# Rotary embedding on one core: TensorE tiles in three groups, a third buffer for the sin product, tables on the queue of x

## The chip, the cores and the metric

The kernel runs on one core of a Trainium2 chip. The core has a matrix engine (TensorE, PE in the profile), a vector engine (VectorE, DVE), a scalar engine (ScalarE, ACT), a general engine (GpSimd, POOL) and SyncE (SP), which here only starts transfers. They share two on-chip memories, SBUF and PSUM; data come from the chip's large memory (HBM) through 16 DMA engines. GpSimd does not touch PSUM in this kernel; TensorE writes only to it. The metric is the device time of one execution in microseconds (us), the median over runs.

## The reference

```python
x: (8, 2048, 8, 64) f32      # batch, position, head, feature
cos, sin: (2048, 32) f32     # one row for each position
x1 = x[..., :32];  x2 = x[..., 32:]
out1 = x1 * cos - x2 * sin   # cos, sin repeated over batch and heads
out2 = x1 * sin + x2 * cos
return concatenate([out1, out2], axis=-1)
```

Each half of a head's 64 features is multiplied by cos, the other half by sin (with a minus sign for the first), and the two products are added. x and the result are 33.55 MB each, the tables 0.26 MB each.

## The kernel before, in words

The 2048 positions are spread over the 128 partitions, 16 to a partition. A *pair* is eight positions of one batch for all partitions (128 x 4096 floats, 2 MB); there are 16 pairs, and each is loaded by one transfer and stored by one. Only the first load and the last store are cut in two. A pair consists of two *tiles* of 128 x 2048 floats, so there are 32 tiles, numbered 0 to 31; pair p holds tiles 2p and 2p + 1. All loads of x are issued by SyncE in the order of the pairs, into a ring of ten pair buffers (xpool). The result is written over x in the same buffer and the store is issued by ScalarE's queue (L155; L151 and L153 for the last two halves), so a buffer comes free for a later load when its store has landed.

The tables are loaded by ScalarE's queue (L56, L57). VectorE makes ssin from sin, once with and once without the minus sign (L80, L81), and copies cos to PSUM (L82); ScalarE copies sin to PSUM (L83). GpSimd makes an identity matrix (eye), ScalarE a negative one (neye).

A tile is done in one of three ways, which the table `kinds` gives by its number:

- **A** (all others): GpSimd makes the sin product t2 in two halves (L118), VectorE the cos product t1 in PSUM (L123), VectorE adds them (L129).
- **B** (6, 9, 14, 16, 21, 27): GpSimd makes t2 as in A, VectorE makes t1 in SBUF (L123); TensorE adds them by multiplying each with the identity into one PSUM buffer (L134, L135), in four chunks of 512; ScalarE copies each chunk to the tile's place (L136).
- **C** (3, 11, 18, 24): VectorE makes both products (L111 for sin, L123 for cos); TensorE adds them with eye or neye and with the halves exchanged (L143, L144); ScalarE copies (L147). GpSimd has no part in it.

The rings: t2 has two SBUF buffers for all kinds; t1 of A has one PSUM buffer; t1 of B and C (tag t1s) has two SBUF buffers; the PSUM chunks o of TensorE have two. A buffer comes free when its last reader is done: the add for A, the last matmuls for B and C.

Order: each engine runs its own queue in order and waits by semaphores. A planner sets the order of every queue when the program is built: it goes by the loop's order, but moves an instruction ahead of one that it expects to wait, and it fixes which buffer each tile gets. So the order in the trace isn't exactly that of the loop, and a wait for a buffer is a wait for one given earlier reader.

Of the kernel before, what the change touches and what calls it, by code (L numbers as in the profile page):

```python
# [2 lines left out]

# [4 lines left out]


@with_exitstack  # L10
def kernel(
    ctx: ExitStack,
    tc: tile.TileContext,
    x: bass.AP,
    cos: bass.AP,
    sin: bass.AP,
    out: bass.AP,
):
    nc = tc.nc
    f32 = mybir.dt.float32  # L20
    PSUM = bass.MemoryType.PSUM

    B, S, H, D = x.shape
    Dh = D // 2
    P = 128
    HD = H * D
    R = S // P

    SL = 4
    FREE = SL * HD  # L30
    PAIR = 2 * FREE
    n_pair = R // (2 * SL)
    C = 512

    xv = x.rearrange("b (q r) h d -> b q (r h d)", q=P)
    ov = out.rearrange("b (q r) h d -> b q (r h d)", q=P)
    cos_src = cos.rearrange("(q r) d -> q r d", q=P)
    sin_src = sin.rearrange("(q r) d -> q r d", q=P)

    const_pool = ctx.enter_context(tc.tile_pool(name="const", bufs=1))  # L40
    tab_pool = ctx.enter_context(tc.tile_pool(name="tab", bufs=1, space=PSUM))
    t1_pool = ctx.enter_context(tc.tile_pool(name="t1p", bufs=1, space=PSUM))
    o_pool = ctx.enter_context(tc.tile_pool(name="op", bufs=2, space=PSUM))
    xpool = ctx.enter_context(tc.tile_pool(name="xpool", bufs=10))
    t1s_pool = ctx.enter_context(tc.tile_pool(name="t1s", bufs=2))
    t2_pool = ctx.enter_context(tc.tile_pool(name="t2p", bufs=2))

    cos_sb = const_pool.tile([P, R, Dh], f32, tag="cb")
    sin_sb = const_pool.tile([P, R, Dh], f32, tag="sb")
    ssin = const_pool.tile([P, R, 2, Dh], f32, tag="ss")  # L50
    eye = const_pool.tile([P, P], f32, tag="eye")
    neye = const_pool.tile([P, P], f32, tag="neye")
    cos_ps = tab_pool.tile([P, R, Dh], f32, tag="cp")
    sin_ps = tab_pool.tile([P, R, Dh], f32, tag="sp")

    nc.scalar.dma_start(out=sin_sb, in_=sin_src)  # L56
    nc.scalar.dma_start(out=cos_sb, in_=cos_src)  # L57

    pairs = [(b, l) for l in range(n_pair) for b in range(B)]
    xts = []  # L60
    for i, (b, l) in enumerate(pairs):
        xt = xpool.tile([P, PAIR], f32, tag="xt", name=f"xt{i}")
        for lo, n in [(0, FREE), (FREE, FREE)] if i == 0 else [(0, PAIR)]:
            nc.sync.dma_start(
                out=xt[:, lo : lo + n],
                in_=xv[b, :, l * PAIR + lo : l * PAIR + lo + n],
            )
        xts.append(xt)

    nc.gpsimd.memset(eye, 0.0)  # L70
    nc.gpsimd.affine_select(
        out=eye,
        in_=eye,
        compare_op=mybir.AluOpType.not_equal,
        fill=1.0,
        base=0,
        pattern=[[-1, P]],
        channel_multiplier=1,
    )
    nc.vector.tensor_scalar_mul(ssin[:, :, 0, :], sin_sb, -1.0)  # L80
    nc.vector.tensor_copy(ssin[:, :, 1, :], sin_sb)  # L81
    nc.vector.tensor_copy(cos_ps, cos_sb)  # L82
    nc.scalar.copy(sin_ps, sin_sb)  # L83
    nc.scalar.mul(neye, eye, -1.0)

    def rep(a, n):
        return dataclasses.replace(a, ap=[a.ap[0][:], a.ap[1][:], [0, n], a.ap[-1][:]])

    kinds = {3: "C", 11: "C", 18: "C", 24: "C", 6: "B", 9: "B", 14: "B", 16: "B", 21: "B", 27: "B"}
    n_tiles = 2 * len(pairs)  # L90

    for i in range(n_tiles):
        b, l = pairs[i // 2]
        pt = xts[i // 2]
        half = i % 2
        xt = pt[:, half * FREE : (half + 1) * FREE]
        r0 = (2 * l + half) * SL
        kind = kinds.get(i, "A")
        xk = xt.rearrange("p (r k d) -> p r k d", r=SL, d=Dh)
        xu = xt.rearrange("p (g u d) -> p g u d", u=2, d=Dh)  # L100

        t2 = t2_pool.tile([P, FREE], f32, tag="t2")
        t2u = t2.rearrange("p (g u d) -> p g u d", u=2, d=Dh)
        if kind == "A":
            t1 = t1_pool.tile([P, FREE], f32, tag="t1")
        else:
            t1 = t1s_pool.tile([P, FREE], f32, tag="t1s")
        t1u = t1.rearrange("p (g u d) -> p g u d", u=2, d=Dh)

        if kind == "C":  # L110
            nc.vector.tensor_mul(  # L111
                out=t2.rearrange("p (r k d) -> p r k d", r=SL, d=Dh),
                in0=xk,
                in1=rep(sin_ps[:, r0 : r0 + SL, :], 2 * H),
            )
        else:
            for u in range(2):
                nc.gpsimd.tensor_mul(  # L118
                    out=t2u[:, :, u, :].rearrange("p (r h) d -> p r h d", h=H),
                    in0=xu[:, :, 1 - u, :].rearrange("p (r h) d -> p r h d", h=H),  # L120
                    in1=rep(ssin[:, r0 : r0 + SL, u, :], H),
                )
        nc.vector.tensor_mul(  # L123
            out=t1.rearrange("p (r k d) -> p r k d", r=SL, d=Dh),
            in0=xk,
            in1=rep(cos_ps[:, r0 : r0 + SL, :], 2 * H),
        )
        if kind == "A":
            nc.vector.tensor_add(out=xt, in0=t1, in1=t2)  # L129
        elif kind == "B":  # L130
            for j in range(FREE // C):
                o = o_pool.tile([P, C], f32, tag="o")
                cs = slice(j * C, (j + 1) * C)
                nc.tensor.matmul(o, eye, t1[:, cs], start=True, stop=False)  # L134
                nc.tensor.matmul(o, eye, t2[:, cs], start=False, stop=True)  # L135
                nc.scalar.copy(xt[:, cs], o)  # L136
        else:
            G = C // Dh
            for u in range(2):
                for j in range(FREE // 2 // C):  # L140
                    o = o_pool.tile([P, C], f32, tag="o")
                    gs = slice(j * G, (j + 1) * G)
                    nc.tensor.matmul(o, eye, t1u[:, gs, u, :], start=True, stop=False)  # L143
                    nc.tensor.matmul(  # L144
                        o, eye if u else neye, t2u[:, gs, 1 - u, :], start=False, stop=True
                    )
                    nc.scalar.copy(xu[:, gs, u, :], o.rearrange("p (g d) -> p g d", d=Dh))  # L147

        base = l * PAIR
        if i == n_tiles - 2:  # L150
            nc.scalar.dma_start(out=ov[b, :, base : base + FREE], in_=xt)  # L151
        elif i == n_tiles - 1:
            nc.scalar.dma_start(out=ov[b, :, base + FREE : base + PAIR], in_=xt)  # L153
        elif half:
            nc.scalar.dma_start(out=ov[b, :, base : base + PAIR], in_=pt)  # L155


# [1 line left out]
_INS = ['x', 'cos', 'sin']  # L159
_OUTS = [((8, 2048, 8, 64), 'float32')]  # L160


# [23 lines left out]
```

## Time and profile before

| | before |
|---|---|
| median of 3 runs | 194.11 us (193.7 to 194.29) |
| the profiled execution | 196.04 us |
| its span, first to last instruction | 194.3 us |
| VectorE busy | 132.9 us (68%) |
| GpSimd busy | 129.7 us (67%) |
| TensorE busy, mean granted clock | 91.8 us (47%), 0.789 |
| ScalarE busy | 25.2 us (13%) |
| bytes moved | 67.68 MB, mean 348 GB/s over the span |

The profile is of one execution. Its page gives busy time by engine; the span in 40 equal slices of 4.86 us with the DMA rate of each; the chain of work that ended last; groups of instructions by source line (busy time, mean, idle time before them and what ended it); and the DMA issues. A line is named L118 for line 118 of the kernel as printed above. In a group's row, `t<-xt,ssin` is what is written and what is read, with buffer numbers left out, so t1 and t2 both appear as t. Busy times that lie beside each other on different engines do not add up; idle time of an engine matters only where the chain passes through it.

### The profile page before, as it was taken

To read this page: it belongs to the slowest core of one execution; us is meant where nothing else is said; L and a number is where in the kernel's file an instruction comes from. 1 tells how busy PE (TensorE), PEld (TensorE's weight loads), DVE (VectorE), ACT (ScalarE), POOL (GpSimd) and SP (SyncE) were. 2 spreads that over 40 slices of the span, in tenths; PEclk is the share of its full clock that TensorE was granted. 3 is DMA by queue.
4 is the path that set the end of the run, shared out by engine and by line. 5 is a ranking of instruction groups with operands and counts; after the bars stand their busy time and mean duration, and the time that the engine had idled before them with its cause. 6 is when DMAs were issued, how large, how long until landed. Compare 5 with 4: busy or idle time off the path is not lost. (4 is left out here: it accounts for less than half of the span.)

```text
span 194.3 us, 670 instructions
## 1 busy us (share of the span) xinstructions
PE 91.8 (47%) x160; PEld 36.2 (19%) x160; DVE 132.9 (68%) x61; ACT 25.2 (13%) x43; POOL 129.7 (67%) x62
## 2 busy tenths in 40 slices
PE   0000009949342999026969991159149508900000
PEld 0000004414011343012424340024024103300000
DVE  0199999981996394994581979906999960955940
ACT  2100001302200222020222231011023101102000
POOL 1599345998659636859598459595972689559900
PEclk9999999996955599855796999658859965885555
DMA  6999999999999999999999999990069950008596
GB/s 208 439 432 428 378 432 432 432 432 432 432 432 432 432 432 432 432 432 432 432 428 428 432 427 428 430 398 7 2 253 418 405 219 0 0 0 378 216 432 270
DMA packets 5189, 67.68 MB, mean 348 GB/s; under 512 B 577, under 2 KB 577, under 8 KB 833
## 3 DMA queue, kind: packets, MB, share of 16 engines
q10 hardware_dynamic: 2736, 34.08, 41.3%
q1 hardware_dynamic: 2448, 33.56, 41.0%
q8 instruction: 1, 0.02, 0.0%
q14 instruction: 4, 0.02, 0.0%
HBM read 34.08 MB, written 33.55 MB: 348 GB/s over the span
## 5 line engine op out<-in xcount | busy, mean ns | idle before, releaser
L118 POOL TENSOR_TENSOR t<-xt,ssin 128x1024 f32<-128x1024 f32 x56 | 129.0, 2332 | 53.8 <-DVE xt L129 39.4
L129 DVE TENSOR_TENSOR xt<-t,t 128x2048 f32<-128x2048 f32 x22 | 50.4, 2292 | 43.8 <-POOL t L118 43.4
L123 DVE TENSOR_TENSOR t<-xt,cos_ps 128x2048 f32<-128x2048 f32 x32 | 72.4, 2290 | 0.6
L135 PE MATMUL o<-t,eye 128*128 128x512 f32 x48 | 33.7, 797 | 23.5 <-POOL t L118 23.5
L134 PE MATMUL o<-t,eye 128*128 128x512 f32 x48 | 32.4, 767 | 18.9 <-DVE t L123 10.6
L143 PE MATMUL o<-t,eye 128*128 128x512 f32 x32 | 19.0, 679 | 35.5 <-DVE t L123 29.0
L136 ACT COPY xt<-o 128x512 f32<-128x512 f32 x24 | 13.8, 586 | 92.1 <-PE o L135 75.2
L135 PEld LDWEIGHTS o<-t,eye 128*128 128x128 f32 x48 | 11.2, 246 | 42.2 <-POOL t L118 29.9
L134 PEld LDWEIGHTS o<-t,eye 128*128 128x128 f32 x48 | 11.5, 251 | 37.1 <-issue 27.0
L147 ACT COPY xt<-o 128x512 f32<-128x512 f32 x16 | 9.3, 586 | 53.7 <-PE o L144 43.2
L143 PEld LDWEIGHTS o<-t,eye 128*128 128x128 f32 x32 | 6.8, 219 | 43.8 <-issue 36.5
L144 PE MATMUL o<-t,neye 128*128 128x512 f32 x16 | 9.7, 696 | 0.5 <-DVE t L111 0.5
L111 DVE TENSOR_TENSOR t<-xt,sin_ps 128x2048 f32<-128x2048 f32 x4 | 9.1, 2287 | 0.3
L144 PE MATMUL o<-t,eye 128*128 128x512 f32 x16 | 8.2, 593 | 0.0
L80 DVE TENSOR_SCALAR ssin<-sin_sb 128x512 f32<-128x512 f32 x1 | 0.4, 427 | 6.6 <-DMA sin_sb<-in_sin_dram 6.6
L144 PEld LDWEIGHTS o<-t,neye 128*128 128x128 f32 x16 | 3.6, 232 | 6.1 <-issue 3.7
L144 PEld LDWEIGHTS o<-t,eye 128*128 128x128 f32 x16 | 3.0, 190 | 3.8 <-issue 3.8
L82 DVE COPY cos_ps<-cos_sb 128x512 f32<-128x512 f32 x1 | 0.7, 695 | 2.4 <-DMA cos_sb<-in_cos_dram 2.4
L83 ACT ACT_TABLE_LOAD x1 | 1.3, 1283 | 1.7 <-PEq L170 1.7
L83 ACT COPY sin_ps<-sin_sb 128x512 f32<-128x512 f32 x1 | 0.6, 590 | 3.7 <-DMA sin_sb<-in_sin_dram 3.7
L81 DVE COPY ssin<-sin_sb 128x512 f32<-128x512 f32 x1 | 0.4, 421 | 0.0
L70 POOL MEMSET eye<- 128x128 f32 x1 | 0.2, 204 | 0.3 <-POOLq L170 0.3
(6 smaller groups left out, 1.0 us busy)
## 6 DMA issues: line engine op xcount, KB each, us to landing
xt<-in_x_dram SPq DMA_DIRECT2D x15, 2048.0 KB, 32.4
out_dram<-xt ACTq DMA_DIRECT2D x15, 2048.0 KB, 14.3
xt<-in_x_dram SPq DMA_DIRECT2D x2, 1024.0 KB, 7.0
out_dram<-xt ACTq DMA_DIRECT2D x2, 1024.0 KB, 5.2
sin_sb<-in_sin_dram ACTq DMA_DIRECT2D x1, 256.0 KB, 5.8
cos_sb<-in_cos_dram ACTq DMA_DIRECT2D x1, 256.0 KB, 8.6
```

Source lines behind the costliest of these rows:

```text
L82: nc.vector.tensor_copy(cos_ps, cos_sb)
L83: nc.scalar.copy(sin_ps, sin_sb)
L111: nc.vector.tensor_mul(out=t2.rearrange("p (r k d) -> p r k d", r=SL, d=Dh), in0=xk, in1=rep(sin_ps[:, r0 : r0 + SL, :], 2 * H),)
L118: nc.gpsimd.tensor_mul(out=t2u[:, :, u, :].rearrange("p (r h) d -> p r h d", h=H), in0=xu[:, :, 1 - u, :].rearrange("p (r h) d -> p r h d" ...
L123: nc.vector.tensor_mul(out=t1.rearrange("p (r k d) -> p r k d", r=SL, d=Dh), in0=xk, in1=rep(cos_ps[:, r0 : r0 + SL, :], 2 * H),)
L129: nc.vector.tensor_add(out=xt, in0=t1, in1=t2)
L134: nc.tensor.matmul(o, eye, t1[:, cs], start=True, stop=False)
L135: nc.tensor.matmul(o, eye, t2[:, cs], start=False, stop=True)
L136: nc.scalar.copy(xt[:, cs], o)
L143: nc.tensor.matmul(o, eye, t1u[:, gs, u, :], start=True, stop=False)
L144: nc.tensor.matmul(o, eye if u else neye, t2u[:, gs, 1 - u, :], start=False, stop=True)
L147: nc.scalar.copy(xu[:, gs, u, :], o.rearrange("p (g d) -> p g d", d=Dh))
```

## The change

The ten TensorE tiles become nine, in three groups of consecutive tiles: a C tile (5, 13, 21) with two B tiles behind it (6, 7; 14, 15; 22, 23). t2 gets a third buffer, and so does the ring t1s; a C tile's sin product takes its buffer from t1s and no longer from t2. The ring of x goes from ten pair buffers to nine. The two table loads are issued by SyncE, ahead of the loads of x, and no longer by ScalarE's queue.

```diff
-    xpool = ctx.enter_context(tc.tile_pool(name="xpool", bufs=10))
-    t1s_pool = ctx.enter_context(tc.tile_pool(name="t1s", bufs=2))
-    t2_pool = ctx.enter_context(tc.tile_pool(name="t2p", bufs=2))
+    xpool = ctx.enter_context(tc.tile_pool(name="xpool", bufs=9))
+    t1s_pool = ctx.enter_context(tc.tile_pool(name="t1s", bufs=3))
+    t2_pool = ctx.enter_context(tc.tile_pool(name="t2p", bufs=3))
...
-    nc.scalar.dma_start(out=sin_sb, in_=sin_src)
-    nc.scalar.dma_start(out=cos_sb, in_=cos_src)
+    nc.sync.dma_start(out=sin_sb, in_=sin_src)
+    nc.sync.dma_start(out=cos_sb, in_=cos_src)
...
-    kinds = {3: "C", 11: "C", 18: "C", 24: "C", 6: "B", 9: "B", 14: "B", 16: "B", 21: "B", 27: "B"}
+    kinds = {}
+    for g in (5, 13, 21):
+        kinds |= {g: "C", g + 1: "B", g + 2: "B"}
...
-        t2 = t2_pool.tile([P, FREE], f32, tag="t2")
+        if kind == "C":
+            t2 = t1s_pool.tile([P, FREE], f32, tag="t1s", name="t2c")
+        else:
+            t2 = t2_pool.tile([P, FREE], f32, tag="t2")
```

## The prediction

> **What bounds the kernel now.** I read the page's head and slices first, then the engines' waits, the timelines of GpSimd, VectorE and TensorE, and last a table of DMA by stretches.
>
> ```profile
> span 194.3 us, 670 instructions
> PE 91.8 (47%) x160; PEld 36.2 (19%) x160; DVE 132.9 (68%) x61; ACT 25.2 (13%) x43; POOL 129.7 (67%) x62
> GB/s 208 439 432 428 378 432 432 432 432 432 432 432 432 432 432 432 432 432 432 432 428 428 432 427 428 430 398 7 2 253 418 405 219 0 0 0 378 216 432 270
> DMA packets 5189, 67.68 MB, mean 348 GB/s; under 512 B 577, under 2 KB 577, under 8 KB 833
> POOL 23%; issue 10%; DVE 9%; POOLq 1%; DVEq 0%
> ```
>
> No engine is busy over 68% of the span. The DMA row is flat near 432 until about 126 us (26 slices of 4.86) and then has holes: in the first part transfers fill the time, in the last third they wait for results. The chain that ended last is GpSimd and VectorE in turn, with 10% "issue" between. Who waits for whom (engine and line, waited for: total us, times, longest):
>
> ```profile
> DVE xt L129 <- POOL t L118: 43.4, 17, 7.0
> POOL t L118 <- DVE xt L129: 39.4, 14, 5.8
> ```
>
> The add (L129) waits for the sin product of its tile (L118), and the next sin product waits for an add. The second wait is a buffer's: t2 has two, and a tile for TensorE holds one for long, so GpSimd and VectorE share the other in turns. In time:
>
> ```profile
> 7.11 13.84 POOL L118 TENSOR_TENSOR t<-xt,ssin 128x1024 f32<-128x1024 f32 x6 [5.81 <-DVE ssin L80]
> 116.69 4.62 POOL L118 TENSOR_TENSOR t<-xt,ssin 128x1024 f32<-128x1024 f32 x2 [2.40 <-DVE xt L129]
> 123.71 9.18 POOL L118 TENSOR_TENSOR t<-xt,ssin 128x1024 f32<-128x1024 f32 x4 [2.40 <-DVE xt L129]
> 15.23 2.29 DVE L123 TENSOR_TENSOR t<-xt,cos_ps 128x2048 f32<-128x2048 f32 x1
> 19.95 2.29 DVE L123 TENSOR_TENSOR t<-xt,cos_ps 128x2048 f32<-128x2048 f32 x1
> 22.16 2.28 DVE L111 TENSOR_TENSOR t<-xt,sin_ps 128x2048 f32<-128x2048 f32 x1
> 24.36 2.28 DVE L129 TENSOR_TENSOR xt<-t,t 128x2048 f32<-128x2048 f32 x1
> 116.65 4.49 DVE L123 TENSOR_TENSOR t<-xt,cos_ps 128x2048 f32<-128x2048 f32 x2
> 121.34 2.29 DVE L129 TENSOR_TENSOR xt<-t,t 128x2048 f32<-128x2048 f32 x1 [0.21 <-POOL t L118]
> ```
>
> Columns: start, length, engine, line, operation, count, idle time before it with its releaser. A tile costs GpSimd 4.62 (two halves). Started alone it goes 116.69 to 123.71, 7.02 a tile: 4.62, then 2.40 for the add. Two facts for later: an ordinary tile costs VectorE 19.95 - 15.23 = 4.72 when multiply and add alternate, two multiplies in a row 4.49; and the instruction order isn't that of the loop: one multiply of a coming TensorE tile (L111 at 22.16, the second L123 at 116.65) stands ahead of an add.
>
> **The change part by part.** *Floor of the transfers.* Bytes stay the same.
>
> ```profile
> 0.00:2.50 2.50, 0.00 (x0) 0.00 (x0) 0.00 (x0) 0.85 (x1) 0.70 (x6) 1.00 0.33 52
> 2.50:122.00 119.50, 64.18 (x114) 25.34 (x114) 87.98 (x42) 17.56 (x31) 83.07 (x36) 0.86 1.01 428
> 192.50:194.30 1.80, 0.00 (x0) 0.00 (x0) 0.00 (x0) 0.00 (x0) 0.00 (x0) 0.50 0.02 5
> ```
>
> The last columns are the granted clock, DMA share and GB/s. From 2.5 us on 428 GB/s, and some 1.7 us after the last bytes. 67.68 MB less 0.13 at 428 is 157.8; with 2.5 and 1.7 the span cannot be below about 162.0. At the flat 432 it is 160.6. The Trainium skill ("DMA: Bandwidth & Descriptors", section Bandwidth) says that between HBM and on-chip memory the HBM side binds, near 358 GB/s; by it 67.68 MB take 189 us and the change could win almost nothing. The trace disagrees: 428 over 119.5 us.
>
> *Groups.* Tiles 3, 11, 18, 24 (C: both products on VectorE) and 6, 9, 14, 16, 21, 27 (B: sin product on GpSimd) become 5, 13, 21 (C) and the two behind each (B): nine instead of ten. GpSimd's products go from 56 to 58, +4.6 us. VectorE keeps 58 large operations (23 x 2 + 3 x 2 + 6, before 22 x 2 + 4 x 2 + 6). TensorE loses 16 matmuls and ScalarE 4 copies: nothing by themselves, with 47% and 13% busy.
>
> *Buffers.* The third t2, and C's sin product moved to the t1s ring (three), so that only B tiles hold t2. Without any waits GpSimd would need 7.1 + 29 x 4.62 = 141.1, the last add 2.3 more: 143.4. VectorE: first add at 7.1 + 4.62 = 11.7, so a start of 9.3; 23 x 4.72 + 6 x 2.25 (C) + 6 x 2.25 (B) = 135.6; end 144.9. VectorE is later, by little.
>
> ```profile
> 184.30 2.29 DVE L129 TENSOR_TENSOR xt<-t,t 128x2048 f32<-128x2048 f32 x1
> 186.63 0.34 ACTq L153 DMA_DIRECT2D out_dram<-xt  x1
> ```
>
> From the last add's end (186.59) to the end of the span it is 7.7 now; so 144.9 + 7.7 = 152.6 plus stalls S. The floor of 162.0 hides the first 9.4 us of S.
>
> *Stalls of a group.* TensorE's time for a tile:
>
> ```profile
> 28.98 2.05 PE L143 MATMUL o<-t,eye 128*128 128x512 f32 x2 [28.98 <-DVE t L123]
> 38.32 1.96 PE L134 MATMUL o<-t,eye 128*128 128x512 f32 x4
> 70.86 1.02 PE L143 MATMUL o<-t,eye 128*128 128x512 f32 x2
> 76.86 1.02 PE L144 MATMUL o<-t,eye 128*128 128x512 f32 x2
> ```
>
> 9.3 after a rest (rows start as 2.05), 7.0 right behind another tile. Take group 5, 6, 7, with time 0 where the add of tile 4 ends, and sin5 ahead of that add, as at 22.16 above. cos5 0 to 2.3; TensorE has tile 5 until 11.6. GpSimd: tile 6 from -2.3 to 2.3, tile 7 to 6.9, tile 8 (third buffer) to 11.5. cos6 to 4.5, cos8 to 6.8; cos7 has no t1s buffer, since tile 5 has two of three until 11.6. Then either add8 first (11.5 to 13.8), or cos7 first (11.6 to 13.9) and add8 to 16.2. Tile 9 wants to start at 11.5, but tiles 6 and 7 hold their t2 (6 leaves TensorE at 18.6, 7 at 25.6), so it starts at add8's end: 13.8 or 16.2. Tile 10 gets tile 6's buffer at 18.6 against 18.4, or has no wait. Loss 2.5 or 4.7 a group, 7.5 or 14.1 for three. If cos5 too is issued behind other work (TensorE until 13.9), the same steps give 4.6 with add8 first, 7.0 with cos7 first, and in the loop's strict order (cos7, cos8, add8) 9.2: 13.8, 21 and 27.6 for three. With both multiplies of C early by one more operation the loss is at most 2.3, 7 for three. Which order is issued no row of before shows. I take 14: one multiply ahead is what the trace has nearly everywhere, and cos7 becomes ready within 0.1 us of add8. Ends: 7 and 28.
>
> Sum: 152.6 + 14 = 166.6, with the floor at 162.0 beneath it.
>
> *Tables ahead of x on SP.*
>
> ```profile
> xt<-in_x_dram SPq DMA_DIRECT2D x15, 2048.0 KB, 32.4
> xt<-in_x_dram SPq DMA_DIRECT2D x2, 1024.0 KB, 7.0
> sin_sb<-in_sin_dram ACTq DMA_DIRECT2D x1, 256.0 KB, 5.8
> cos_sb<-in_cos_dram ACTq DMA_DIRECT2D x1, 256.0 KB, 8.6
> 0.73 0.40 ACTq L56 DMA_DIRECT2D sin_sb<-in_sin_dram  x1
> 19.95 0.35 ACTq L155 DMA_DIRECT2D out_dram<-xt  x1
> 9.78 0.69 DVE L82 COPY cos_ps<-cos_sb 128x512 f32<-128x512 f32 x1 [2.41 <-DMA cos_sb<-in_cos_dram]
> ```
>
> Now the tables share the engines with x and cos lands last, so VectorE's first multiply is at 10.5. Two issues (some 0.4 us each) and 0.52 MB (1.2 us at 428) go ahead of x's first half: it lands up to 2.0 later than now, or no later, since those bytes also competed with it before. GpSimd's start: 7.1, bounds 6 to 9. VectorE starts 2 to 3 us sooner, but its first add waits for GpSimd at 11.7 (now 12.9). I take 0 beyond the 11.7 that is in the sum. ScalarE's queue loses two issues that nothing waited behind.
>
> *Ring of x from 10 to 9.* Pair 9's load now waits for pair 0's store (now issued at 19.95); GpSimd reaches pair 9 near 7.1 + 16 x 4.62 = 81, some 60 us later: I take nothing, unless loads come late at the end. With both queues sharing 432, a pair takes 9.7 us; from some 20 us (four pairs in) twelve more end near 136. Pair 15 then needs 2 x 4.62 + 2.3 and the tail of 7.7: 155, under the floor. If that cover goes, each us late counts fully beyond 162.
>
> **The rivals.**
>
> ```profile
> L118 POOL TENSOR_TENSOR t<-xt,ssin 128x1024 f32<-128x1024 f32 x56 | 129.0, 2332 | 53.8 <-DVE xt L129 39.4 <-issue 8.4 <-DVE ssin L80 5.8
> ACT xt L147 <- DVE xt L129: 10.5, 1, 10.5
> ACT xt L136 <- DVE xt L129: 16.9, 2, 8.7
> ```
>
> (1) Transfers bind alone: S stays under 9.4, and the span is 162. For it: 26 flat slices, two waits of 40 us attacked. Against: S must be 3 a group or less. (2) cos7 stands ahead of add8 while TensorE is still on tile 5: S 21 to 28, span 173 to 180. For it: tile 5 takes two of three t1s buffers, and a resting TensorE needs 9.3. Against: multiplies are seen moved forward, around waits. (3) Slower: B tiles hold the added buffer as well. TensorE gets three tiles in a row, 9.3 + 7.0 + 7.0, so two of three t2 are held much of the time, and every other tile goes at 7.02. If GpSimd's idle time behind the start stays as it is (53.8 less 5.8), the 4.6 of the added tile come on top: 194.3 + 4.6 = 199. It decides from 42 us of idle on. Against: by the steps above both are held only from 2.3 to 18.6 in a group of 37 us, two tiles' worth. (4) The two other rows: three times ScalarE's copies stood 8 to 10.5 behind a store that waited for an add, and TensorE with them. Once in each group on the way to tile 6's release, up to 10.5 more a group: 166.6 + 31 = 198, no gain. Against it: the store behind a group (tiles 8 and 9) comes after that group's copies in the loop. (5) The rate falls to the span's mean of 348 with loads and stores mixed throughout: 67.68/0.348 + 4.2 = 199. Against it: the kernel mixes them from 20 us on without a fall. The 358 of the Trainium skill's DMA page would give 193 in the same way.
>
> **How the numbers follow.** The forecast, S between 9.4 and 18, is 0.42 and spans 162 to 171. Rival 1 is 0.24, rival 2 is 0.23, rivals 3 and 4 are 0.04 each, rival 5 is 0.03. Predicted: 166.6 on the span. The profiled execution took 196.04 with a span of 194.3; the median of the runs, 194.11, is 0.2 under the span, so 166.4. The range goes from 160.5 (flat 432) to 179 (rival 2) and leaves out rivals 3 to 5 (0.11) and the worst of rival 2, some 0.15 together. About 0.3% is what a measurement here can tell from no change. Faster: forecast, rivals 1 and 2, a part of 4: 0.91. Same 0.02, slower 0.07.
>
> **What would show it.** GpSimd's waits for L129 fall from 39.4 to under 15, and what is left stands behind tiles 8, 16 and 24. DMA stays near 430 until past 150 us. VectorE has no wait for L118 over 3 us outside the groups. L118 shows x58 with the same 2.33 us. cos_ps is copied before 7 us. The prediction is wrong if 7.02 remains the pace of ordinary tiles, if L123 shows idle time for TensorE over 5 us a group, or if DMA has holes with x still to be loaded.

## The result and the profile after

The changed kernel takes 176.36 us (median of 4 runs, 175.32 to 177.09) against 194.2 us for the kernel before in the same series: a ratio of 0.9065, 95% interval 0.8993 to 0.9136. It is 17.8 us faster, and 10.0 us slower than the 166.4 that was forecast, inside the range of 160.5 to 179. Medians are over all runs of a version and ratios over its fast runs; of the four runs of each version that has all stores on SyncE (below) one was slow, which raises its median by 0.4 to 0.6 us.

In the changed kernel the lines have other numbers: L123 is GpSimd's sin product, L128 VectorE's cos product, L134 the add, L139, L140 and L141 the two matmuls and the copy of a B tile, L148, L149 and L152 those of a C tile, L160 a store. In the changed kernel with the old tile numbers they are two lower (L121 for the sin product, L132 for the add). From the page of the changed kernel: the head, busy time by engine, the DMA rate in 40 slices of 4.38 us, the chain.

```profile
span 175.3 us, 632 instructions
PE 79.5 (45%) x144; PEld 32.4 (18%) x144; DVE 132.7 (76%) x61; ACT 22.5 (13%) x39; POOL 134.0 (76%) x64
GB/s 176 331 443 426 426 378 445 419 430 430 441 434 422 426 434 445 426 430 422 437 441 419 434 421 437 441 419 428 430 432 437 366 202 0 419 60 359 419 419 239
POOL 58%; issue 18%; DVE 14%; DMA 4%; SPq 0%; DVEq 0%; POOLq 0%
```

Busy time is what it was: VectorE 132.7 (132.9 before), GpSimd 134.0 (129.7, one more tile). The rate is flat until 136 us (31 slices) and holes come only then. So the gain is idle time between GpSimd and VectorE. The longest waits of the changed kernel (who, for what: us in total, times, longest):

```profile
ACT xt L141 <- DVE xt L134: 68.0, 7, 10.7
PE o L139 <- ACT xt L141: 37.7, 6, 7.8
POOL t L123 <- DVE xt L134: 21.2, 6, 7.5
DVE xt L134 <- POOL t L123: 15.4, 8, 2.4
DVE t L128 <- PE o L148: 9.5, 3, 5.1
```

GpSimd's waits for an add fell from 39.4 to 21.2, VectorE's for a sin product from 43.4 to 15.4. New are VectorE's wait for TensorE (a buffer of t1s) and, at the head of the list, ScalarE's copies behind something that waits for an add: 68.0 in seven waits, three waits with 27.4 before. The timeline of GpSimd, whole from the first product on:

```profile
9.58 36.59 POOL L123 TENSOR_TENSOR t<-xt,ssin 128x1024 f32<-128x1024 f32 x16 [8.27 <-DMA xt<-in_x_dram]
53.66 4.63 POOL L123 TENSOR_TENSOR t<-xt,ssin 128x1024 f32<-128x1024 f32 x2 [7.50 <-DVE xt L134]
60.69 27.77 POOL L123 TENSOR_TENSOR t<-xt,ssin 128x1024 f32<-128x1024 f32 x12 [2.40 <-DVE xt L134]
92.59 4.60 POOL L123 TENSOR_TENSOR t<-xt,ssin 128x1024 f32<-128x1024 f32 x2 [4.13 <-DVE xt L134]
99.60 27.77 POOL L123 TENSOR_TENSOR t<-xt,ssin 128x1024 f32<-128x1024 f32 x12 [2.40 <-DVE xt L134]
129.77 4.59 POOL L123 TENSOR_TENSOR t<-xt,ssin 128x1024 f32<-128x1024 f32 x2 [2.40 <-DVE xt L134]
136.77 27.51 POOL L123 TENSOR_TENSOR t<-xt,ssin 128x1024 f32<-128x1024 f32 x12 [2.40 <-DVE xt L134]
```

In four of the seven stretches it now makes six or eight tiles without a stop, where 7.02 a tile was the pace before. Two waits are left behind each group: 7.50 and 2.40, 4.13 and 2.40, 2.40 and 2.40. The first group on VectorE, TensorE and ScalarE:

```profile
37.11 2.28 DVE L134 TENSOR_TENSOR xt<-t,t 128x2048 f32<-128x2048 f32 x1
39.31 2.28 DVE L128 TENSOR_TENSOR t<-xt,cos_ps 128x2048 f32<-128x2048 f32 x1
46.70 4.49 DVE L128 TENSOR_TENSOR t<-xt,cos_ps 128x2048 f32<-128x2048 f32 x2 [5.10 <-PE o L148]
51.29 2.29 DVE L134 TENSOR_TENSOR xt<-t,t 128x2048 f32<-128x2048 f32 x1
...
37.34 2.05 PE L148 MATMUL o<-t,eye 128*128 128x512 f32 x2 [37.34 <-DVE t L128]
45.64 1.02 PE L148 MATMUL o<-t,eye 128*128 128x512 f32 x2
53.36 1.02 PE L140 MATMUL o<-t,eye 128*128 128x512 f32 x2
61.66 2.08 PE L139 MATMUL o<-t,eye 128*128 128x512 f32 x2 [5.56 <-ACT xt L141]
75.29 1.92 PE L140 MATMUL o<-t,eye 128*128 128x512 f32 x2
...
60.65 0.34 ACTq L160 DMA_DIRECT2D out_dram<-xt  x1
61.03 1.07 ACT L141 COPY xt<-o 128x512 f32<-128x512 f32 x2 [7.74 <-DVE xt L134]
72.40 0.34 ACTq L160 DMA_DIRECT2D out_dram<-xt  x1
72.78 1.07 ACT L141 COPY xt<-o 128x512 f32<-128x512 f32 x2 [10.69 <-DVE xt L134]
```

TensorE starts on tile 5 at 37.34, before add4 is over (39.39). After cos6 (39.31) VectorE stands until TensorE has read cos5 for the last time (45.64 and 1.02 more); then come cos7 and cos8 (46.70, two multiplies), then add8 (51.29), which releases the buffer for tile 9 at 53.66. GpSimd had been done with tile 8 at 46.17. TensorE is done with tile 6 at 54.4, but tile 10 starts at 60.69, when add9 is over: the planner had given it tile 9's buffer, not tile 6's, which had been free for 4 us when GpSimd was done with tile 9 at 58.29. The semaphores in the trace bear this out: tile 10's product waits for VectorE's, tile 11's for TensorE's. And tile 7, begun at 54.2, stays on TensorE until 77, because its chunks' copies stand on ScalarE's queue behind two stores (60.65, 72.40) that wait for the adds of tiles 9 and 11.

### The profile page after: what moved, and what is told of

It reads as the page before. It is cut to its first block, busy times and chain, and to the rows that moved or that the text cites. A ratio compares the mean times of both kernels' runs of the same rounds, so it can differ in the third digit from the quotient of the medians.

```text
span 175.3 us, 632 instructions
## 1 busy us (share of the span) xinstructions
PE 79.5 (45%) x144; PEld 32.4 (18%) x144; DVE 132.7 (76%) x61; ACT 22.5 (13%) x39; POOL 134.0 (76%) x64
## 4 chain that ended last, share of the span: by engine, by line
POOL 58%; issue 18%; DVE 14%; DMA 4%; SPq 0%; DVEq 0%; POOLq 0%
POOL t L123 58%; DVE xt L134 8%; DVE t L128 7%; DMA xt<-in_x_dram 4%; SPq L57 0%; SPq L56 0%; DVEq L134 0%; POOLq L123 0%
## 5 line engine op out<-in xcount | busy, mean ns | idle before, releaser
L123 POOL TENSOR_TENSOR t<-xt,ssin 128x1024 f32<-128x1024 f32 x58 | 133.3, 2342 | 29.7 <-DVE xt L134 21.2
L128 DVE TENSOR_TENSOR t<-xt,cos_ps 128x2048 f32<-128x2048 f32 x32 | 72.8, 2291 | 14.8 <-PE o L148 9.5
L134 DVE TENSOR_TENSOR xt<-t,t 128x2048 f32<-128x2048 f32 x23 | 52.7, 2290 | 16.6 <-POOL t L123 15.4
L139 PE MATMUL o<-t,eye 128*128 128x512 f32 x48 | 32.7, 771 | 37.7 <-ACT xt L141 37.7
L148 PE MATMUL o<-t,eye 128*128 128x512 f32 x24 | 14.6, 695 | 37.6 <-DVE t L128 37.6
L140 PE MATMUL o<-t,eye 128*128 128x512 f32 x48 | 29.5, 702 | 0.0
L141 ACT COPY xt<-o 128x512 f32<-128x512 f32 x24 | 13.4, 588 | 83.4 <-DVE xt L134 68.0
L139 PEld LDWEIGHTS o<-t,eye 128*128 128x128 f32 x48 | 10.9, 242 | 53.5 <-ACT xt L141 42.8
L140 PEld LDWEIGHTS o<-t,eye 128*128 128x128 f32 x48 | 11.3, 236 | 15.9 <-issue 15.9
L152 ACT COPY xt<-o 128x512 f32<-128x512 f32 x12 | 7.0, 586 | 51.3 <-PE o L149 51.3
L148 PEld LDWEIGHTS o<-t,eye 128*128 128x128 f32 x24 | 5.1, 224 | 45.2 <-POOL t L123 37.3
L149 PE MATMUL o<-t2c,neye 128*128 128x512 f32 x12 | 7.5, 713 | 0.0
L116 DVE TENSOR_TENSOR t2c<-xt,sin_ps 128x2048 f32<-128x2048 f32 x3 | 6.8, 2280 | 0.0
L149 PE MATMUL o<-t2c,eye 128*128 128x512 f32 x12 | 6.1, 592 | 0.0
L149 PEld LDWEIGHTS o<-t2c,neye 128*128 128x128 f32 x12 | 2.9, 239 | 4.1 <-issue 4.1
L149 PEld LDWEIGHTS o<-t2c,eye 128*128 128x128 f32 x12 | 2.3, 190 | 2.9 <-issue 2.9
```

Source lines behind the costliest of these rows:

```text
L116: nc.vector.tensor_mul(out=t2.rearrange("p (r k d) -> p r k d", r=SL, d=Dh), in0=xk, in1=rep(sin_ps[:, r0 : r0 + SL, :], 2 * H),)
L123: nc.gpsimd.tensor_mul(out=t2u[:, :, u, :].rearrange("p (r h) d -> p r h d", h=H), in0=xu[:, :, 1 - u, :].rearrange("p (r h) d -> p r h d" ...
L128: nc.vector.tensor_mul(out=t1.rearrange("p (r k d) -> p r k d", r=SL, d=Dh), in0=xk, in1=rep(cos_ps[:, r0 : r0 + SL, :], 2 * H),)
L149: nc.tensor.matmul(o, eye if u else neye, t2u[:, gs, 1 - u, :], start=False, stop=True)
```

## The experiments

The theory after the result: the third t2 buffer brings the gain, and the forecast's gap is the wait for a t1s buffer inside a group (VectorE's 9.5 and what follows). Its rivals: the grouping brings the gain; the gap is due to buffers fixed to the wrong reader, to the stores on ScalarE's queue, or to the start.

**Two t2 buffers again.**

```diff
-    t2_pool = ctx.enter_context(tc.tile_pool(name="t2p", bufs=3))
+    t2_pool = ctx.enter_context(tc.tile_pool(name="t2p", bufs=2))
```

> The changed kernel with two t2 buffers again; C's sin product stays in the t1s ring. Theory (the third t2 buffer carries the gain): the two B tiles of a group hold both buffers, so the tile behind them waits until TensorE leaves the first B tile, some 12 to 14 us later, and the next tile 2.4 more: about 15 us a group in place of the 4.8 to 9.9 seen, so 194 to 200 us, and GpSimd's waits for buffers 42 to 50 us in place of 21. Rival (grouping and the separate place of C's product carry it): 176 to 180.

192.51 us, ratio to before 0.9881 (0.9807 to 0.9956). The gain is nearly all gone, and the rival is wrong; the time is 1.5 us below the theory's range. GpSimd's stop in the first group, TensorE's last row of tile 6, and all three stops together:

```profile
54.00 4.66 POOL L123 TENSOR_TENSOR t<-xt,ssin 128x1024 f32<-128x1024 f32 x2 [10.03 <-issue]
52.84 1.02 PE L140 MATMUL o<-t,eye 128*128 128x512 f32 x2
POOL t L123 <- issue: 29.8, 3, 10.0
```

One stop of some 10 us a group, and 2.4 more behind it: 12.4 in place of the 15 expected. The profile names no releaser, but the first stop ends at 54.00, just after TensorE's last matmul of tile 6 (53.86): the wait is the theory's, and a little shorter.

**Scattered tiles, all buffers as changed.**

```diff
-    kinds = {}
-    for g in (5, 13, 21):
-        kinds |= {g: "C", g + 1: "B", g + 2: "B"}
+    kinds = {3: "C", 11: "C", 18: "C", 24: "C", 6: "B", 9: "B", 14: "B", 16: "B", 21: "B", 27: "B"}
```

> The changed kernel with the tile numbers of before (4 C and 6 B, spread out), all buffers as changed. Theory (the buffers carry the gain, a scattered B tile holds one of three): GpSimd has two buffers left nearly always, 56 products, so 168 to 176 us. Rival (the grouping carries it): 185 to 194.

166.8 us, ratio 0.8555 (0.8483 to 0.8628): the lowest median of all versions, below the theory's range, 9.6 us below the changed kernel, and the intervals of the two ratios are apart. So the grouping doesn't carry the gain. The edit changes two things, though: the tiles are scattered, and TensorE has ten in place of nine, which spares GpSimd one tile (4.6 us). Nine scattered tiles were not tried, so how much of the 9.6 us is the grouping's own is not shown. Its DMA row, its chain and what GpSimd waits for in it:

```profile
GB/s 178 372 435 432 439 372 388 439 428 420 432 439 439 432 424 424 435 435 439 428 420 428 439 434 424 424 428 437 441 428 420 428 439 439 190 384 443 406 418 253
DMA 62%; POOL 12%; PE 9%; DVE 4%; issue 2%; ACT 1%; POOLq 1%; SPq 0%; ACTq 0%; DVEq 0%
POOL t L121 <- DMA xt<-in_x_dram: 15.8, 6, 8.3
POOL t L121 <- DVE xt L132: 4.5, 2, 2.4
```

The rate has one hole, in slice 35, and GpSimd now waits for x (8.3 of it at the start) and hardly for adds, and 62% of the chain that ended last are transfers: they are the bound. The span is 165.5, 3.5 above the floor of 162.0 in the prediction.

**The same with two t2 buffers, and the kernel before with three.** The first leaves C's own place with the third t1s buffer, the ring of x and the tables of the change, the second only the third t2 buffer (and nine of x).

```diff
 # scattered tiles, buffers as changed
-    t2_pool = ctx.enter_context(tc.tile_pool(name="t2p", bufs=3))
+    t2_pool = ctx.enter_context(tc.tile_pool(name="t2p", bufs=2))
 # the kernel before
-    xpool = ctx.enter_context(tc.tile_pool(name="xpool", bufs=10))
+    xpool = ctx.enter_context(tc.tile_pool(name="xpool", bufs=9))
...
-    t2_pool = ctx.enter_context(tc.tile_pool(name="t2p", bufs=2))
+    t2_pool = ctx.enter_context(tc.tile_pool(name="t2p", bufs=3))
```

> The changed kernel with the tile numbers of before and two t2 buffers: what is left of the change is C's product in the t1s ring of three, nine buffers of x, and the tables on SyncE. Theory (the third t2 and C's own place only work together): 185 to 194. Rival (with scattered tiles, taking C out of the ring is most of the gain): 170 to 178.

> The kernel before with three t2 buffers and nine of x, C's sin product still in the t2 ring, two t1s buffers. Theory (the third t2 buffer alone carries the gain, since scattered TensorE tiles hold one at a time): 167 to 173 us. Rival (C's product must leave the ring, since it ties GpSimd's buffers to VectorE's order): 178 to 188.

193.14 us, ratio 0.9893 (0.9818 to 0.9969), and 192.22 us, ratio 0.9825 (0.9778 to 0.9871). Each alone brings 1 to 2%, together they bring 14%. The theory that the third buffer alone does it has fallen, and its rival's 178 to 188 is missed as well; that the two only work together holds. Whether it is C's own place that counts beside the third t2 buffer, or the third t1s buffer that came with it, was not separated. In order, GpSimd's waits for adds without the third buffer, and GpSimd's and ScalarE's with it alone:

```profile
POOL t L121 <- DVE xt L132: 40.0, 16, 4.5
...
POOL t L118 <- DVE xt L129: 39.3, 11, 7.4
ACT xt L147 <- DVE xt L129: 52.1, 3, 23.8
```

Both keep some 40 us of GpSimd's waits, against 4.5 with both parts. In the kernel before with three t2 buffers, copies of C tiles stand up to 23.8 behind a store, and a C tile holds a t2 buffer all that time; that this is what uses up the third buffer is argued from these rows, not tried by itself.

**The groups in the kernel before.** Only `kinds` as in the changed kernel.

```diff
-    kinds = {3: "C", 11: "C", 18: "C", 24: "C", 6: "B", 9: "B", 14: "B", 16: "B", 21: "B", 27: "B"}
+    kinds = {}
+    for g in (5, 13, 21):
+        kinds |= {g: "C", g + 1: "B", g + 2: "B"}
```

> The kernel before with the three groups as its tile numbers and nothing else. Theory (grouping is a loss, which the buffers outweigh): two t2 buffers, a C tile and two B tiles in a row that all want them, so 198 to 212. Rival (grouping helps by itself, since fewer tiles see a held buffer): 182 to 192.

202.05 us, ratio 1.0364 (1.0289 to 1.0438). Grouping, with the one tile more for GpSimd, costs 3.6% here, some 7 us, where it was 9.6 among the new buffers. With them the table is complete: scattered 195 and grouped 202 with the old buffers, 166.8 and 176.4 with the new. But the cost does not come with the groups everywhere: with C's own place and two t2 buffers the two ways take 193.14 and 192.51, with all stores on SyncE (below) 169.62 and 168.71.

**Tables on ScalarE's queue again.**

```diff
-    nc.sync.dma_start(out=sin_sb, in_=sin_src)
-    nc.sync.dma_start(out=cos_sb, in_=cos_src)
+    nc.scalar.dma_start(out=sin_sb, in_=sin_src)
+    nc.scalar.dma_start(out=cos_sb, in_=cos_src)
```

> The changed kernel with the tables loaded by ScalarE's queue as before. Theory (the tables ahead of x cost the start): GpSimd starts at 7.1 in place of 9.6 and all behind it moves, 173.9 us in place of 176.4. Rival (the start is absorbed by the later waits for TensorE, which doesn't start before 37 us): 176 us. VectorE's first multiply moves from 9.5 to 10.5 in both.

175.67 us, ratio 0.9025 (0.8966 to 0.9083), not distinguishable from the changed kernel. GpSimd's first and second stretch, and VectorE's first multiply and add:

```profile
7.33 36.69 POOL L123 TENSOR_TENSOR t<-xt,ssin 128x1024 f32<-128x1024 f32 x16 [6.03 <-DVE ssin L80]
52.84 4.63 POOL L123 TENSOR_TENSOR t<-xt,ssin 128x1024 f32<-128x1024 f32 x2 [8.82 <-DVE xt L134]
11.00 2.30 DVE L128 TENSOR_TENSOR t<-xt,cos_ps 128x2048 f32<-128x2048 f32 x1
13.40 2.29 DVE L134 TENSOR_TENSOR xt<-t,t 128x2048 f32<-128x2048 f32 x1
```

GpSimd starts 2.25 sooner and waits 1.32 longer in the first group: tile 9 comes 0.82 sooner, as VectorE's first add does (13.40, 14.21 in the changed kernel). The rival is right: GpSimd's later start is taken up by the wait that follows, and what sets the first group is VectorE.

**Four t1s buffers, and the control.** To make room the ring of x goes to eight; the control is that alone.

```diff
-    xpool = ctx.enter_context(tc.tile_pool(name="xpool", bufs=9))
-    t1s_pool = ctx.enter_context(tc.tile_pool(name="t1s", bufs=3))
+    xpool = ctx.enter_context(tc.tile_pool(name="xpool", bufs=8))
+    t1s_pool = ctx.enter_context(tc.tile_pool(name="t1s", bufs=4))
```

> The changed kernel with four t1s buffers, and eight pair buffers of x to make room. Theory (the wait of the second B tile's multiply for a t1s buffer is what the forecast had too small): VectorE's waits for TensorE of 5.1 + 2.3 + 2.0 go, add8 comes sooner and tile 9 too, so about 167 to 169 us. Rival (the buffers of t2 that the planner fixes set the pace): VectorE's wait turns into one for GpSimd, 2.4 us remain behind each add of tiles 8, 9 and so on, 172 to 176.

> The changed kernel with eight pair buffers of x and nothing else; the control for the runs with four buffers elsewhere. If the ring of x is hidden: 176 to 177 us, and the four t1s buffers themselves made the last run slow. If the ring is what made it slow: 182 to 184, with loads issued later and DMA holes before 140 us.

The control has 175.49 us, ratio 0.8964 (0.8901 to 0.9027): the ring of x is hidden even at eight. With four t1s buffers it is 184.22 us, ratio 0.9448 (0.9378 to 0.9517), 16 us above the forecast of the theory, above the rival's too, and 8.7 above the control. VectorE's waits for TensorE are gone, as expected. GpSimd's first wait with four t1s buffers and in the control, then waits with four:

```profile
47.43 4.64 POOL L123 TENSOR_TENSOR t<-xt,ssin 128x1024 f32<-128x1024 f32 x2 [2.40 <-DVE xt L134]
52.35 4.63 POOL L123 TENSOR_TENSOR t<-xt,ssin 128x1024 f32<-128x1024 f32 x2 [7.10 <-DVE xt L134]
POOL t L123 <- DVE xt L134: 26.4, 11, 2.4
ACT xt L152 <- DVE xt L134: 30.0, 2, 15.7
```

In the first group the theory holds: tile 9 waits 2.40 and no longer 7.10, less by the 4.70 that VectorE waits for TensorE in the control. But GpSimd now waits 2.4 eleven times, where the changed kernel has six waits, four of them of 2.4: behind the second and the third group it makes several tiles in a row at the old pace of 7.02. The planner had arranged the queues anew, and copies of C tiles, which wait for no add in the changed kernel, now stand up to 15.7 behind a store. That these stops make the B tiles behind them hold their t2 buffers, and so bring the old pace back, is read from the rows and not tried. The t1s wait is thus no independent cost of 9 us; taking it away changed the order, and the new order is slower.

**Four t2 buffers.** Eight of x, as in the control.

```diff
-    xpool = ctx.enter_context(tc.tile_pool(name="xpool", bufs=9))
+    xpool = ctx.enter_context(tc.tile_pool(name="xpool", bufs=8))
...
-    t2_pool = ctx.enter_context(tc.tile_pool(name="t2p", bufs=3))
+    t2_pool = ctx.enter_context(tc.tile_pool(name="t2p", bufs=4))
```

> The changed kernel with four t2 buffers, and eight pair buffers of x to make room. Theory (two B tiles in a row leave GpSimd one buffer of three): tile 9 no longer waits for add8, GpSimd's waits for adds fall from 21.2 to under 8 us, 164 to 168 us by the transfers or VectorE. Rival (VectorE's waits for TensorE, 9.5, delay all the same): VectorE still stands 5 us in the first group, 170 to 173.

167.99 us, ratio 0.8583 (0.854 to 0.8625). The theory's time, though not quite its waits; GpSimd's for adds, and VectorE's for TensorE, which have not gone:

```profile
POOL t L123 <- DVE xt L134: 11.3, 4, 5.2
DVE t L128 <- PE o L148: 11.8, 3, 4.1
```

**Stores on SyncE.** Three lines, all of the form

```diff
-            nc.scalar.dma_start(out=ov[b, :, base : base + PAIR], in_=pt)
+            nc.sync.dma_start(out=ov[b, :, base : base + PAIR], in_=pt)
```

> The changed kernel with all stores issued by SyncE and none by ScalarE. Theory (ScalarE's copies stand behind stores that wait for adds, 68.0 us in 7 waits, TensorE with them, 37.7, and tile 7 keeps its t2): these waits go, tile 7 leaves TensorE 7 to 15 us sooner, and the 2.4 us waits that follow go where tile 7's buffer is used: 168 to 172 us. Rival (what follows tile 7 doesn't need its buffer by then): 175 to 177. If loads get stuck behind stores on SyncE: over 178 with DMA holes while x is still being loaded.

168.71 us, ratio 0.8569 (0.8501 to 0.8637). GpSimd's stretches behind the first, and TensorE's last row of the first group:

```profile
53.58 32.13 POOL L123 TENSOR_TENSOR t<-xt,ssin 128x1024 f32<-128x1024 f32 x14 [7.38 <-DVE xt L134]
90.99 32.16 POOL L123 TENSOR_TENSOR t<-xt,ssin 128x1024 f32<-128x1024 f32 x14 [5.29 <-DVE xt L134]
126.86 32.06 POOL L123 TENSOR_TENSOR t<-xt,ssin 128x1024 f32<-128x1024 f32 x14 [3.71 <-DVE xt L134]
60.14 1.02 PE L140 MATMUL o<-t,eye 128*128 128x512 f32 x2
```

Tile 7 leaves TensorE at 61 in place of 77, ScalarE waits for no add, and the second wait of each group, 2.40, is gone; the first stays (7.38, 5.29 and 3.71 against 7.50, 4.13 and 2.40). So the second wait comes with the stores on ScalarE's queue, and the first does not. The expectation named tile 7's buffer for this, but tile 10 starts before tile 7 has left TensorE. By the semaphores tile 10's product now waits for TensorE: it has tile 6's buffer. TensorE was done with tile 6 at some 54 in both kernels, so what the edit changed is the planner's choice; why the stores' place leads to it is open.

**Both parts together, and stores on SyncE with scattered tiles.** The edits are those above, combined.

> The changed kernel with four t2 buffers, eight of x, and all stores issued by SyncE. If the fourth buffer (168.0) and the freed copies (168.7) each take away the same waits of GpSimd, the two together give 165 to 168, no more than the better one. If they take away different ones, 162 to 164, at the floor of the transfers.

> The changed kernel with the tile numbers of before and all stores issued by SyncE. Theory (with scattered tiles 166.8 is already the transfers' time, with GpSimd waiting for x): freed copies win nothing, 165 to 167, or loads that stand behind stores on SyncE lose some, 168 to 172. Rival (its three waits of ScalarE for adds, 32.9 us, still cost): 162 to 164.

169.83 us, ratio 0.8694 (0.8617 to 0.8772), and 169.62 us, ratio 0.8679 (0.8602 to 0.8757). The first is above both expectations: the two gains don't add. In the second nothing is won for the scattered tiles, and by the median some is lost, as one branch of the expectation had it, though the intervals still touch. The DMA rows of the two:

```profile
GB/s 175 309 442 428 424 436 432 424 432 436 424 432 420 409 350 409 428 420 436 381 428 436 401 401 333 430 432 432 424 370 436 432 424 428 432 424 432 426 414 89
GB/s 157 315 437 427 427 431 435 435 427 435 419 372 427 431 439 423 439 435 427 415 364 427 435 437 431 345 429 431 411 352 435 439 435 423 435 415 435 435 419 94
```

Neither has a hole: transfers run from the first slice to the last. In the second the last add is over at 146.6, 21 us before the end, so there the transfers come last; in the first it is over at 161.4, 7.1 before the end, and what binds it is not settled. With everything on one queue the rate dips to 333 to 372 in several slices. The lowest median stays 166.8, of the scattered tiles with the new buffers; the groups with four t2 buffers (167.99) or with the stores on SyncE (168.71) can't be told from it, since the intervals overlap.

## Why the prediction was right, and where it was wrong

- **The direction and the main mechanism** (buffers of t2 let GpSimd run on; VectorE and GpSimd stay as busy as before): right. GpSimd's stretches of 12 and 16 halves show it, and without the third buffer the time is 192.5. What the prediction did not separate: with the third buffer alone, or with C's own place and its third t1s buffer alone, only 1 to 2% is won. The span of 175.3 is past the 162 to 171 of the forecast's own case and inside rival 2's 173 to 180.
- **The stalls, 14 for three groups**: mis-sized. GpSimd waits 21.2 for adds. The first waits of the groups, 7.50, 4.13 and 2.40, add up to 14.0, which is luck. Rival 2's order came (cos7 and cos8 ahead of add8, as in the loop), but cos5 stood one operation earlier than in the forecast, and add8 ended 14.2 after add4, near the 13.8 of the best case. GpSimd waited 7.50 all the same, because with the third buffer it was further ahead: done with tile 8 at 6.8 after add4, and not at 11.5. The rest, 3 x 2.40 = 7.2, are the second waits, so rival 2's bracket was hit in part by something that is not in rival 2.
- **The step that failed** is "Tile 10 gets tile 6's buffer at 18.6 against 18.4, or has no wait". The planner gave it tile 9's, and the wait is 2.40 in every group. Behind it stands the dismissal of rival 4: "the store behind a group (tiles 8 and 9) comes after that group's copies in the loop". In the loop, yes; on ScalarE's queue the planner had put it ahead of the last copy of tile 6. ScalarE waited 68.0 us in seven waits. Its price was not 10.5 a group on the way to tile 6's release, which came in time, but the second waits and a late end: moving the stores brought 7.7 us by the medians, and 8.1 in the profiles, 5.3 up to the last add and 2.8 behind it.
- **The grouping** got no price against scattered tiles: in "Groups" only counts of operations were compared. With the tile less on TensorE it costs 9.6 us with the new buffers and some 7 with the old ones. That is as much as the whole gap, though it comes by the waits above and is not to be added to them.
- **Tables ahead of x**, taken as nothing: right in time, wrong in place. GpSimd starts at 9.58, outside the bounds of 6 to 9, since x's first half lands later; putting the tables back brought 0.7 us by the medians, which is within the noise, because the wait that follows takes the start up.
- **From span to median**: the 0.2 was the wrong step, worth 1.3. In both profiles the execution took 1.7 to 1.8 more than its span; the profiled execution of before was merely 1.9 above its median. Here the median is 1.1 above the span.
- **The floor of 162**: not reached by any run; the shortest span is 163.5, in profiles 165.5, both with the scattered tiles. The Trainium skill's 358 GB/s ("DMA: Bandwidth & Descriptors", section Bandwidth), by which next to nothing could be won, does not bind here, with one core at work: this kernel moves 419 to 445 in most slices while loads and stores are mixed.
- **Account of the 10.0**, by VectorE's first and last add:

```profile
14.21 2.29 DVE L134 TENSOR_TENSOR xt<-t,t 128x2048 f32<-128x2048 f32 x1 [2.38 <-POOL t L123]
165.25 2.29 DVE L134 TENSOR_TENSOR xt<-t,t 128x2048 f32<-128x2048 f32 x1
```

The last add ends at 167.54 where the sum had 158.9, which is 8.6 later: the first add starts 2.5 later than the 11.7 of the sum, and from there on VectorE takes 153.3 where the sum had 147.2 (133.2 of work and the 14), 6.1 more. The median brings 1.3 and the tail 0.1. Of the 2.5 only 0.8 goes with the tables' place: that much sooner the first add starts with them on ScalarE's queue.

What was to be seen in the trace: a DMA rate that is flat past 150 us did not come (136), nor waits for adds under 15 (21.2). Three of the six waits left stand behind tiles 8, 16 and 24, the other three behind 9, 17 and 25. VectorE's waits for a sin product stay under 3, and idle time before a multiply for TensorE is just over the 5 that was named, in one group (5.10).

## What to carry to other kernels

A buffer more helps only if the operations that hold buffers longest don't take it too: here a third buffer, and a place in another, larger ring for the product that TensorE reads late, brought 1 to 2% each and 14% together. Before engine work is grouped, count how many buffers the group holds at a time against the same work scattered; the scattered one, with one tile more on TensorE, won by 9.6 us, and the groups came up to it with a fourth t2 buffer, or with no store before the copies. An edit of one ring or one queue can change the planner's order elsewhere (a fourth t1s buffer made the kernel 8.7 us slower), so read the whole order again after each. And look at what stands in front of the copies on a queue that also issues stores: a store that waits for another engine stops them, and a planner that goes by expected times can put it there although the loop doesn't.

## What was not expected of the hardware

- With the tables on SyncE ahead of x, GpSimd started on x's first half only at 7.7 to 10.0 us in ten profiles, held by x; with the tables on ScalarE's queue it started at 7.1 to 7.5 in four, held by the table. The second slice has 304 to 426 GB/s in the ten and 437 to 451 in the four. The slices differ in length from run to run; in stretches of 2 us the changed kernel moves 303 and 315 GB/s from 4 to 8 us, the kernel before 427 and 436. Why the start is slower with the tables ahead on one queue is open.
- With loads and stores all on SyncE's queue, slices of 333 to 372 GB/s appear in mid-run, which runs with two queues don't show between their first slices and their first hole, but for one or two slices near 25 us. SyncE then also stands between its issues, for adds 31.2 us in four waits with the groups and three t2 buffers, so whether the one queue or the order of the issues makes the dips is open.
